# GpSimd's two-input products cut into 256-column pieces, and another order for the second pass of the latent out projection

## The chip, the cores and the metric

The kernel runs on one core of a Trainium2 chip. A core has TensorE (PE, matrix products and transposes), VectorE (DVE), ScalarE (ACT), GpSimd (POOL) and SyncE (SP, which here issues the loads and stores); each works through its own list of instructions and waits for others by semaphores. The metric is the time of one execution on the device in microseconds (us), the median of several.

## The reference

Two transformer blocks of two layers each, in fp32, on 512 tokens of width 1024 (the second block also has 256 context tokens).

```python
# first block: pooling mixer, then stick-breaking attention; after each, x += (p @ ple_w) * sigmoid(x @ ple_gate_w)
u, z = split(rms_norm(x) @ a_w_in)              # windows of 2, 4, 8, 16 tokens over u, minus u
x = x + (einsum(pooled, w_group) * scale * silu(z)) @ a_w_out
k, v = split(rms_norm(x) @ w_kv); q, z = split(rms_norm(x) @ b_w_in)
a[t, s] = beta[t, s] * prod(1 - beta[t, j] for s < j < t)     # beta = sigmoid(q.k / 8), causal
x = x + ((a @ v) * silu(z)) @ b_w_out
# second block: latent attention (layer 0, tokens and context), differential attention (layer 1, tokens only)
shift, scale, gate = adaln(c, ada_w[i], ada_b[i])             # the context has its own, from c_ctx
h = x * (1 + scale) + shift
x = layer_norm(ALPHA * x + gate * (o @ out_w[i]), ln_g[i], ln_b[i])
ctx = layer_norm(ALPHA * ctx + gate_c * (o_c @ out_w[i]), ...)   # in layer 0 alone
```

## The kernel before

**Products and weights.** Every fp32 product is three reduced-precision products: a weight unit of 128 partitions x 1024 columns (512 KB, usually four 128-row slices of the contraction by 256 columns) is loaded into `wraw` (three buffers), ACT casts it to `wh` (L126) and GpSimd subtracts to get the rest `wl` (L127); both have four buffers. `mm3` then issues wh x h, wh x l and wl x h (L147 to L149). `w()` hands out the next unit of a planned list (`plan`) and with that lets the loads run three units and the splits two units ahead. Activations are split the same way: ACT casts, DVE subtracts (L233, L234).

**Stages.** Layer 0 (pooling mixer) runs to about 250 us, the key and value projection to 380, the first block's attention to about 545, the out projection, the latent layer's products and its attention to 1045; the latent out projection with its layer norm (`ln0`) takes the time from 1045 to 1180, differential attention that to 1530, and the last out projection the rest. In the pooling mixer DVE sums windows (L446), scales (L449) and corrects the first tokens (L451); its outputs are the next products' right sides.

**Stick-breaking attention.** Per pair of heads three tiles of scores are made (`first`, L695 on). ACT takes two sigmoids, DVE runs a scan backwards along each segment (L712; a tile of 1024 columns has segments of 512, 384 and 128 columns), GpSimd multiplies the scan by beta (L715, one product of 1023 columns, or two of 255 for the third tile), PE transposes the result (`aT_p`), DVE or ACT evacuates it (`aT`, L733), PE multiplies by the values.

**Latent out projection (`ln0`, L1155; `out_ln`, L1115).** Pass 1 makes the outputs of the context (`c`, two token blocks) and of tokens 0 and 1 (`0`), pass 2 those of tokens 2 and 3 (`1`). Each pass goes through four groups of 256 columns (`cg` 0 to 3), two weight units each, so the same eight units are loaded, cast and split twice. Per group DVE multiplies the sums by the gate (L1140) and adds the residual `r` (L1141, with the row sum); after the last group the layer norm follows (L1147 to L1151, the inverse root in `rsqrt`, L199 to L204). `done` writes tokens back as the residual of the next layer (L1179, L1180; DVE for `0`, GpSimd for `1`). `next_acts` transposes the normalized rows (`hT_p`, two transposes to a 256-column tile), DVE applies the modulation (`hm`, L1189), and `split` makes the next layer's activations `hc`, `h0`, `h1`. For `c` and `0` it is handed to pass 2 as `fill`, called behind each group; for `1` it follows pass 2.

**Gates.** `ada_piece` makes the modulation in 48 small pieces placed through the program; its part 2 writes the gate without bias to DRAM. `gate_rows` (L811 to L818) loads gate and bias, each spread over 128 partitions, and adds them, on GpSimd for the latent layer, on DVE for the last.

**What sets the order.** A scheduler puts each engine's instructions in order ahead of time, by priorities that go by program order, and moves later ones forward where its own model finds an engine waiting. Buffers come from pools with a fixed number of buffers, so a write waits for the last reader of its buffer.

## Time and profile before

| | us |
|---|---|
| median of three runs | 1586.16 (1583.03 to 1586.99) |
| the profiled execution | 1584.99 |
| its span | 1583.2 |
| PE busy in the span | 1488.9 |
| DVE, ACT, POOL busy | 925.2, 733.7, 603.4 |

The profile is of one execution; its span goes from the first to the last instruction, and 1.8 us lie around it. Matmuls overlap in PE's pipeline, so a row's duration of one matmul (0.28 us) is more than the time from one to the next (0.12 us). "Idle" ahead of a row is the time in which the engine had nothing to run, and the name behind the arrow is what it waited for last. [...]

### The profile page before, as it was taken

What the parts mean: (1) busy time and instruction counts of PE and PEld (TensorE: products, weight loads), DVE (VectorE), ACT (ScalarE), POOL (GpSimd) and SP (SyncE); (2) the same over time, 40 slices, a digit from 0 to 9 for tenths busy, and PEclk for the clock granted to TensorE, in tenths of its full rate; (3) what the DMA queues carried; (4) which work ended last, traced back from release to release, by engine and by line L of the source; (5) the groups of instructions that cost most, each with busy time, mean ns of one, the idle gap of its engine ahead of it and who ended that gap; (6) DMA issues with size and microseconds to landing.
All of it is one profiled execution on the core that took longest, in us unless ns stands there. A gap on an engine that the chain in (4) does not pass through costs nothing.

```text
span 1583.2 us, 24444 instructions
## 1 busy us (share of the span) xinstructions
PE 1488.9 (94%) x9590; PEld 1247.9 (79%) x9590; DVE 925.2 (58%) x1769; ACT 733.7 (46%) x1347; POOL 603.4 (38%) x431
## 2 busy tenths in 40 slices
PE   6999999999899899999999999997897999999997
PEld 4777889998555578888876667577797989999987
DVE  6676465532776656442465665547857655555576
ACT  5323344435666433332565555533335553555642
POOL 2533555643544453222333332444342424343310
PEclk9999999999999999999999999999899999999999
DMA  5323432323344334311103030434321112121122
GB/s 168 90 77 93 127 119 75 101 87 98 102 134 134 106 120 124 90 44 50 51 1 116 9 120 2 146 120 164 117 81 44 41 41 68 41 66 43 54 77 97
DMA packets 149747, 136.01 MB, mean 86 GB/s; under 512 B 12612, under 2 KB 135224, under 8 KB 149632
## 3 DMA queue, kind: packets, MB, share of 16 engines
q1 hardware_dynamic: 149632, 134.45, 27.4%
q8 instruction: 76, 1.25, 0.3%
q14 instruction: 39, 0.32, 0.1%
HBM read 126.02 MB, written 8.40 MB: 85 GB/s over the span
## 4 chain that ended last, share of the span: by engine, by line
PE 40%; DVE 7%; ACT 5%; issue 3%; DMA 2%; POOL 1%; SPq 0%; DVEq 0%; POOLq 0%; ACTq 0%
PE PT_p L172 4%; PE pv L1076 3%; PE qkv_p L147 2%; PE qkv_p L149 2%; PE qkv_p L148 2%; PE pv L1440 2%; PE gt_p L147 2%; PE gt_p L148 2%; PE gt_p L149 2%; PE lg L147 2%; PE lg L148 1%; ACT pe L1095 1%; PE lg L149 1%; DVE st L1094 1%; PE ada_p L787 1%
## 5 line engine op out<-in xcount | busy, mean ns | idle before, releaser
L127 POOL TENSOR_TENSOR wl<-wraw,wh 128x1024 fp32r<-128x1024 f32 (+2 forms) x159 | 377.0, 2380 | 377.9 <-ACT wh L126 364.8
L126 ACT CAST wh<-wraw 128x1024 fp32r<-128x1024 f32 (+2 forms) x164 | 166.3, 1020 | 282.1 <-issue 60.7
L1095 ACT ACTIVATE pe<-lg,st 128x768 f32<-128x768 f32 x160 | 130.5, 817 | 71.6 <-DVE st L1094 55.4
L1094 DVE TENSOR_REDUCE st<-lg 128x1 f32<-128x768 f32 x160 | 133.5, 843 | 38.8 <-PE lg L1421 20.1
L1055 POOL TENSOR_SCALAR pe<-pe,st 128x768 f32<-128x768 f32 (+1 forms) x96 | 73.4, 768 | 145.8 <-DVE st L1096 130.1
L147 PE MATMUL qkv_p<-wh,h 128*128 128x256 f32 x384 | 109.5, 285 | 0.9 <-ACT V L1366 0.7
L172 PE MATMUL PT_p<-ident,pe 128*128 128x128 f32 x640 | 99.6, 279 | 9.5 <-DVE pe L1426 3.3
L149 PE MATMUL qkv_p<-wh,h 128*128 128x256 f32 x384 | 108.1, 282 | 0.2 <-DVE h L234 0.2
L148 PE MATMUL qkv_p<-wl,h 128*128 128x256 f32 x384 | 108.1, 282 | 0.0
L172 PEld LDWEIGHTS PT_p<-ident,pe 128*128 128x128 f32 x640 | 72.6, 141 | 39.9 <-issue 16.9
L1425 POOL TENSOR_SCALAR pe<-pe,st 128x768 f32<-128x768 f32 x32 | 29.2, 912 | 126.7 <-DVE st L1424 85.5
L147 PE MATMUL out_p<-wh,o 128*128 128x256 f32 x256 | 74.5, 292 | 0.9 <-DVE y L1292 0.8
L147 PEld LDWEIGHTS qkv_p<-wh,h 128*128 128x128 f32 x384 | 72.5, 189 | 3.4 <-ACT V L1366 1.3
L148 PE MATMUL out_p<-wl,o 128*128 128x256 f32 x256 | 73.7, 290 | 1.4 <-POOL wl L127 1.4
L149 PE MATMUL out_p<-wh,o 128*128 128x256 f32 x256 | 73.5, 291 | 0.1
L147 PE MATMUL kv_p<-wh,kv 128*128 128x256 f32 x256 | 72.2, 282 | 1.2 <-ACT kv L236 1.2
L149 PEld LDWEIGHTS qkv_p<-wh,h 128*128 128x128 f32 x384 | 72.4, 189 | 0.4 <-DVE h L234 0.4
L148 PEld LDWEIGHTS qkv_p<-wl,h 128*128 128x128 f32 x384 | 72.6, 189 | 0.0
L148 PE MATMUL kv_p<-wl,kv 128*128 128x256 f32 x256 | 71.6, 280 | 0.0
L715 POOL TENSOR_TENSOR sb_b<-sb_b,sb_k 128x1023 f32<-128x1023 f32 (+1 forms) x32 | 43.0, 1355 | 74.2 <-DVE sb_k L712 44.9
L149 PE MATMUL kv_p<-wh,kv 128*128 128x256 f32 x256 | 71.2, 280 | 0.0
L712 DVE TENSOR_TENSOR_SCAN sb_k<-sb_k 128x512 f32<-128x512 f32 (+3 forms) x64 | 61.2, 996 | 10.4 <-ACT sb_k L707 10.3
(456 smaller groups left out, 4545.6 us busy)
## 6 DMA issues: line engine op xcount, KB each, us to landing
araw<-in_ada_w_dram SPq DMA_DIRECT2D x48, 512.0 KB
wraw<-in_diff_w_in_dram SPq DMA_DIRECT2D x32, 512.0 KB
wraw<-in_out_w_dram SPq DMA_DIRECT2D x24, 512.0 KB
wraw<-in_a_w_in_dram SPq DMA_DIRECT2D x16, 512.0 KB
...
```

What stands on the lines that cost most here:

```text
L126: nc.scalar.copy(h[:, :n], raw[:, :n])
L127: (nc.vector if i < 3 or pool == "ow3" else nc.gpsimd).tensor_tensor(out=l[:, :n], in0=raw[:, :n], in1=h[:, :n].bitcast(F32), op=ALU.subtract)
L147: mm(out, lhsT=lh, rhs=rh, start=start, stop=False)
L148: mm(out, lhsT=lh, rhs=rl, start=False, stop=False)
L149: mm(out, lhsT=ll, rhs=rh, start=False, stop=stop)
L172: self.nc.tensor.transpose(out, in_, self.ident[:in_.shape[0], :in_.shape[0]])
L712: nc.vector.tensor_tensor_scan(out=kp[:, rev], data0=kp[:, rev], data1=kp[:, rev], initial=1.0, op0=ALU.mult, op1=ALU.min)
L715: nc.gpsimd.tensor_tensor(out=bt[:, o:o + w - 1], in0=bt[:, o:o + w - 1], in1=kp[:, o + 1:o + w], op=ALU.mult)
L1055: nc.gpsimd.tensor_scalar(out=pe, in0=pe, scalar1=st[:, 1:2], scalar2=0.0, op0=ALU.mult, op1=ALU.add)
L1076: return nc.tensor.matmul(pv[64 * ee:64 * ee + 64, :], lhsT=V[:, k0 + k, vs], rhs=HH[px][:, k, :], start=(k == 0), stop=(k == nk - 1))
L1094: nc.vector.tensor_reduce(out=st[:, 0:1], in_=L, axis=AX.X, op=ALU.max, negate=True)
L1095: nc.scalar.activation(pe, L, AF.Exp, bias=st[:, 0:1], accum_out=st[:, 2:3])
```

## The change

It has three parts. (A) A helper `pool_tt` issues a GpSimd two-input operation as pieces of at most 256 columns. It is used for the weight splits (L127), the gate products (L225), a sum of squares (L500) and the stick product (L715); not for GpSimd's other two-input operations (L528, L1000, L1353, L1179, L1180). (B) The gate's bias is loaded into the small row of `ada_piece` and added there by DVE, which copied there before; `gate_rows` keeps only its load. (C) In `ln0` the residual is loaded straight into `y`, the gated sum goes to a small tile `gp`, and `yc`, `y0`, `y1` and the square's target `sq` have buffers of their own. Pass 2 runs through cg 3, 2, 1, 0: the units of cg 3 and 2 are kept from pass 1 (`held`), so 12 units are loaded in place of 16. `fill` now names the group and token block behind which something is called; each call's transposes are tied to that place on PE (`keep_in_program_order`) for all of `c` and the first four chunks of `0`. `hm` is made by ACT. The scaling of `lng` and `lnb` stands in `affine`, called inside pass 1 behind its group 2; since the loop there runs over both streams, it is called twice. The write-back of `0` and `1` moves behind the transposes (`residual`).

```diff
             nc.scalar.copy(h[:, :n], raw[:, :n])
-            (nc.vector if i < 3 or pool == "ow3" else nc.gpsimd).tensor_tensor(out=l[:, :n], in0=raw[:, :n], in1=h[:, :n].bitcast(F32), op=ALU.subtract)
+            if i < 3 or pool == "ow3":
+                nc.vector.tensor_tensor(out=l[:, :n], in0=raw[:, :n], in1=h[:, :n].bitcast(F32), op=ALU.subtract)
+            else:
+                self.pool_tt(l[:, :n], raw[:, :n], h[:, :n].bitcast(F32), ALU.subtract)
             u["hl"] = (self._w_view(h, u["shape"]), self._w_view(l, u["shape"]))
...
+    def pool_tt(self, out, in0, in1, op):
+        for c in range(0, out.shape[1], 256):
+            cs = slice(c, min(c + 256, out.shape[1]))
+            self.nc.gpsimd.tensor_tensor(out=out[:, cs], in0=in0[:, cs], in1=in1[:, cs], op=op)
...
-        self.nc.gpsimd.tensor_tensor(out=out, in0=sg, in1=z, op=ALU.mult)
+        self.pool_tt(out, sg, z, ALU.mult)
...
-                nc.gpsimd.tensor_tensor(out=ssacc, in0=ssacc, in1=sq, op=ALU.add)
+                self.pool_tt(ssacc, ssacc, sq, ALU.add)
...
             for o, w in ((0, 1024),) if len(segs) == 3 else ((0, 256), (512, 256)):
-                nc.gpsimd.tensor_tensor(out=bt[:, o:o + w - 1], in0=bt[:, o:o + w - 1], in1=kp[:, o + 1:o + w], op=ALU.mult)
+                self.pool_tt(bt[:, o:o + w - 1], bt[:, o:o + w - 1], kp[:, o + 1:o + w], ALU.mult)
             if n == 1 and "next" in h:
...
             nc.tensor.matmul(pr[:4, :], lhsT=self.asel, rhs=row[:, :512], start=True, stop=True)
-            nc.vector.tensor_copy(out=row[:4, 512:], in_=pr[:4, :])
+            for b in range(2):
+                nc.sync.dma_start(out=row[2 * b:2 * b + 2, 512:], in_=self.a["ada_b_2"][layer, 2048 + 512 * b:2560 + 512 * b].partition_broadcast(2))
+            nc.vector.tensor_tensor(out=row[:4, 512:], in0=pr[:4, :], in1=row[:4, 512:], op=ALU.add)
             for b in range(2):
...
         g = pool.tile([P, D], F32, name=f"gate{layer}{v}")
-        b = pool.tile([P, D], F32, tag="res_n", name="gate_b")
-        eng = nc.vector if layer else nc.gpsimd
         nc.sync.dma_start(out=g, in_=self.gates[layer, v].rearrange("a b -> (a b)").partition_broadcast(P))
-        nc.sync.dma_start(out=b, in_=self.a["ada_b_2"][layer, 2048:3072].partition_broadcast(P))
-        eng.tensor_tensor(out=g, in0=g, in1=b, op=ALU.add)
         return g
...
             units.append(self.w_cols(WQ, g * 384, 384))
-        for ps in range(2):
-            for cg in range(4):
-                units += self.w_half(a["out_w_2"][0], cg * 256)
+        for cg in (0, 1, 2, 3, 1, 0):
+            units += self.w_half(a["out_w_2"][0], cg * 256)
         return units
...
-    def out_ln(self, streams, pool, done, fill=()):
-        fill = list(fill)
-        per = -(-len(fill) // 4)
+    def out_ln(self, streams, pool, done, cgs, held, fill={}):
...
         for tag, acts, tbs, res, fac, gate in streams:
-            buf = "0" if tag == "0" else "1"
-            y = {t: pool.tile([P, D], F32, tag="y" + buf, name="y" + buf, bufs=len(tbs)) for t in tbs}
-            r = {t: pool.tile([P, D], F32, tag="r" + buf, name="r" + buf, bufs=len(tbs)) for t in tbs}
+            y = {t: pool.tile([P, D], F32, tag="y" + tag, name="y" + tag, bufs=len(tbs)) for t in tbs}
             st = {t: self.small("lnst", 16, 6) for t in tbs}
             for t in tbs:
-                nc.sync.dma_start(out=r[t], in_=res[t * P:(t + 1) * P, :])
-            ys.append((y, r, st))
-        for cg in range(4):
-            ws = [self.w(), self.w()]
+                nc.sync.dma_start(out=y[t], in_=res[t * P:(t + 1) * P, :])
+            ys.append((y, st))
+        for n, cg in enumerate(cgs):
+            ws = held.pop(cg, None) or [self.w(), self.w()]
+            if n >= 2 and cg >= 2:
+                held[cg] = ws
             cs = slice(cg * 256, (cg + 1) * 256)
-            for (tag, acts, tbs, res, fac, gate), (y, r, st) in zip(streams, ys):
+            for (tag, acts, tbs, res, fac, gate), (y, st) in zip(streams, ys):
                 for i in range(0, len(tbs), 2):
...
                     pp = self.p_mm("out_p")
-                    self.tm(ws, acts, pair[0], len(pair), pp, 256)
+                    for j in range(len(pair)):
+                        self.tm(ws, acts, pair[j], 1, pp[:, j * 256:(j + 1) * 256], 256)
+                        for f in fill.get((n, j), ()):
+                            f()
                     for j, t in enumerate(pair):
                         yt = y[t][:, cs]
-                        nc.vector.tensor_tensor(out=yt, in0=pp[:, j * 256:(j + 1) * 256], in1=gate[:, cs], op=ALU.mult)
-                        nc.vector.scalar_tensor_tensor(out=yt, in0=r[t][:, cs], scalar=fac, in1=yt, op0=ALU.mult, op1=ALU.add, accum_out=st[t][:, 4 + cg:5 + cg])
-            for f in fill[cg * per:(cg + 1) * per]:
-                f()
-        for (tag, acts, tbs, res, fac, gate), (y, r, st) in zip(streams, ys):
+                        gp = pool.tile([P, 256], F32, tag="gp", name="gp", bufs=3)
+                        nc.vector.tensor_tensor(out=gp, in0=pp[:, j * 256:(j + 1) * 256], in1=gate[:, cs], op=ALU.mult)
+                        nc.vector.scalar_tensor_tensor(out=yt, in0=yt, scalar=fac, in1=gp, op0=ALU.mult, op1=ALU.add, accum_out=st[t][:, 4 + cg:5 + cg])
+        for (tag, acts, tbs, res, fac, gate), (y, st) in zip(streams, ys):
             for t in tbs:
...
                 nc.vector.tensor_scalar(out=s[:, 1:2], in0=s[:, 0:1], scalar1=-1.0 / D, scalar2=None, op0=ALU.mult)
-                nc.scalar.activation(r[t], y[t], AF.Square, bias=s[:, 1:2], accum_out=s[:, 2:3])
+                sq = pool.tile([P, D], F32, tag="sq", name="sq", bufs=1)
+                nc.scalar.activation(sq, y[t], AF.Square, bias=s[:, 1:2], accum_out=s[:, 2:3])
                 rs = self.rsqrt(s[:, 2:3], 1, 1.0 / D)
...
         lb = pool.tile([P, D], F32, name="lnb")
-        for t, src in ((lg, a["ln_g_2"]), (lb, a["ln_b_2"])):
-            nc.sync.dma_start(out=t, in_=src[0].partition_broadcast(P))
-            nc.gpsimd.tensor_scalar(out=t, in0=t, scalar1=ALPHA, scalar2=0.0, op0=ALU.mult, op1=ALU.add)
+        def affine():
+            for t, src in ((lg, a["ln_g_2"]), (lb, a["ln_b_2"])):
+                nc.sync.dma_start(out=t, in_=src[0].partition_broadcast(P))
+                nc.gpsimd.tensor_scalar(out=t, in0=t, scalar1=ALPHA, scalar2=0.0, op0=ALU.mult, op1=ALU.add)
...
         def done(s, t, y):
-            rows.setdefault(s, []).append(y)
-            if s != "c":
+            rows.setdefault(s, []).append((t, y))
+        def residual(s):
+            for t, y in rows[s]:
                 r = pool.tile([P, D], F32, tag="res_n", name="res_n", bufs=1)
...
-        def next_acts(s, v, dst, res):
+        def next_acts(s, v, dst, res, held=0):
             def chunk(c):
                 pr = self.p_tr("hT_p")[:, :256]
-                for i, y in enumerate(rows[s]):
-                    self.transpose(pr[:, i * P:(i + 1) * P], y[:, c * P:(c + 1) * P])
+                for i, (t, y) in enumerate(rows[s]):
+                    ins = self.nc.tensor.transpose(pr[:, i * P:(i + 1) * P], y[:, c * P:(c + 1) * P], self.ident)
+                    if c < held and i == 0:
+                        self.tc.keep_in_program_order(ins)
                 hm = pool.tile([P, 256], F32, tag="hm2", name="hm2", bufs=3)
-                nc.vector.tensor_scalar(out=hm, in0=pr, scalar1=gs[v][:, c:c + 1], scalar2=bs[v][:, c:c + 1], op0=ALU.mult, op1=ALU.add)
+                nc.scalar.activation(hm, pr, AF.Identity, scale=gs[v][:, c:c + 1], bias=bs[v][:, c:c + 1])
                 res.append(self.split(hm, dst, "h" + s, n=256))
...
         h0, h1, hc = self.h2_acts = [], [], []
-        self.out_ln([("c", oc_acts, [0, 1], a["ctx_2"][0], ALPHA, gc), ("0", o_acts, [0, 1], self.xs, 1.0, gx)], pool, done)
+        held = {}
+        self.out_ln([("c", oc_acts, [0, 1], a["ctx_2"][0], ALPHA, gc), ("0", o_acts, [0, 1], self.xs, 1.0, gx)], pool, done, (0, 1, 2, 3), held, {(2, 0): [affine]})
+        self.w_advance(self.w_next + 3, self.w_next + 2)
         self.plan(self.diff_units())
-        self.out_ln([("1", o_acts, [2, 3], self.xs, 1.0, gx)], pool, done, next_acts("c", 1, "hc2", hc) + next_acts("0", 0, "hx2", h0))
+        fc, f0 = next_acts("c", 1, "hc2", hc, NK), next_acts("0", 0, "hx2", h0, 4)
+        fill = {(1 + i // 2, i % 2): (fc + f0)[2 * i:2 * i + 2] for i in range(6)}
+        self.out_ln([("1", o_acts, [2, 3], self.xs, 1.0, gx)], pool, done, (3, 2, 1, 0), held, fill)
+        for f in f0[4:]:
+            f()
+        residual("0")
         for f in next_acts("1", 0, "hx2", h1):
             f()
+        residual("1")
         self.close("ln0", "og2s")
```

On POOL, where the stick products begin (`sb_b`) behind the last splits (`wl`) of the query and gate weights. Before:

```order
L127 TENSOR_TENSOR wl<-wraw,wh 128x1024 x7
L715 TENSOR_TENSOR sb_b<-sb_b,sb_k 128x1023 x2
L715 TENSOR_TENSOR sb_b<-sb_b,sb_k 128x255
L225 TENSOR_TENSOR og<-sz,og 128x512
L715 TENSOR_TENSOR sb_b<-sb_b,sb_k 128x255
L715 TENSOR_TENSOR sb_b<-sb_b,sb_k 128x1023 x2
```

After (L144 is the line in `pool_tt`):

```order
L144 TENSOR_TENSOR wl<-wraw,wh 128x256 x28
L144 TENSOR_TENSOR sb_b<-sb_b,sb_k 128x256 x3
L144 TENSOR_TENSOR sb_b<-sb_b,sb_k 128x255
L144 TENSOR_TENSOR sb_b<-sb_b,sb_k 128x256 x3
L144 TENSOR_TENSOR sb_b<-sb_b,sb_k 128x255 x2
L144 TENSOR_TENSOR og<-sz,og 128x256
L144 TENSOR_TENSOR sb_b<-sb_b,sb_k 128x255
L144 TENSOR_TENSOR og<-sz,og 128x256
L144 TENSOR_TENSOR sb_b<-sb_b,sb_k 128x256 x3
```

The long product became three pieces of 256 and one of 255 columns, each with its own wait for the scans; a gate product `og` was split in two with a stick product between.

On PE, at transposes of the normalized context rows inside pass 2 (the numbers tell tiles apart; `out_p` is the out projection's sum, `hT_p` the transposes). Before, the first place:

```order
L147 MATMUL out_p_10276<-wh_10266,o_9653 128x256
L148 MATMUL out_p_10276<-wl_10267,o_9653 128x256
L149 MATMUL out_p_10276<-wh_10266,o_9653 128x256
L172 MATMUL hT_p_10329<-ident_99,y1_9710 128x128
L172 MATMUL hT_p_10329<-ident_99,y1_9711 128x128
L172 MATMUL hT_p_10337<-ident_99,y1_9710 128x128
L172 MATMUL hT_p_10337<-ident_99,y1_9711 128x128
L147 MATMUL out_p_10373<-wh_10272,o_9632 128x256
L148 MATMUL out_p_10373<-wl_10273,o_9632 128x256
```

After, the second place:

```order
L158 MATMUL out_p_10719<-wh_10332,o_10016 128x256
L1201 MATMUL hT_p_10784<-ident_99,yc_10063 128x128 [waits Activation_49]
L1201 MATMUL hT_p_10784<-ident_99,yc_10064 128x128
L1201 MATMUL hT_p_10792<-ident_99,yc_10063 128x128 [waits Activation_49]
L1201 MATMUL hT_p_10792<-ident_99,yc_10064 128x128
L156 MATMUL out_p_10919<-wh_10808,o_9995 128x256 [waits Activation_49]
L157 MATMUL out_p_10919<-wl_10809,o_9995 128x256 [waits Pool_49]
L158 MATMUL out_p_10919<-wh_10808,o_9995 128x256
L156 MATMUL out_p_10919<-wh_10808,o_9998 128x256
L157 MATMUL out_p_10919<-wl_10809,o_9998 128x256 [waits Pool_49]
L156 MATMUL out_p_10719<-wh_10477,o_9995 128x256 [waits DVE_49]
L157 MATMUL out_p_10719<-wl_10478,o_9995 128x256
```

Before, the transposes stand behind 48 products of the pass and come again after 11, 30 and 7 products; now the first four stand behind 72, these four behind 24 more, and so on, with the products of cg 1 and 0 behind them. `wl_10809` is a unit of cg 0 and the third that is split after the kept ones; its first five products stand ahead of those of cg 1 (`wl_10478`).

On DVE before, where the first context chunk comes out of the transposes (`hm`, then the subtraction `hc`):

```order
L1151 TENSOR_SCALAR y_9718<-y_9718,lnst,rs_y 128x1024
L204 SCALAR_TENSOR_TENSOR rs_y<-rs_t,rs_y 128x1
L1189 TENSOR_SCALAR hm_10332<-hT_p,gs_9701,bs_9703 128x256
L1179 TENSOR_TENSOR res_n<-y_9718,lng 128x1024
L1151 TENSOR_SCALAR y_9719<-y_9719,lnst,rs_y 128x1024
L1180 TENSOR_TENSOR res_n<-res_n,lnb 128x1024
L234 TENSOR_TENSOR hc<-hm_10332,hc 128x256
L1189 TENSOR_SCALAR hm_10340<-hT_p,gs_9701,bs_9703 128x256
L1189 TENSOR_SCALAR hm_10348<-hT_p,gs_9701,bs_9703 128x256
```

and on ACT after, where that chunk now is:

```order
L126 CAST wh<-wraw 128x1024
L210 ACTIVATE rs_y<-rs_y 128x1
L209 ACTIVATE rs_y<-rs_m 128x1
L126 CAST wh<-wraw 128x1024
L210 ACTIVATE rs_y<-rs_y 128x1
L1205 ACTIVATE hm_10747<-hT_p,bs_10056,gs_10054 128x256
L1205 ACTIVATE hm_10755<-hT_p,bs_10056,gs_10054 128x256
L242 CAST hc<-hm_10747 128x256
L242 CAST hc<-hm_10755 128x256
L126 CAST wh<-wraw 128x1024 x2
```

The evacuation left DVE's list, where residual additions (`res_n`) stood on both sides of it, for ACT's, where it stands behind two weight casts and ahead of two more; the subtraction stays on DVE.

## Rows read from the trace of the kernel before

**Rows 1.** the page's part 1: busy time, share of the span, instructions
```profile
PE 1488.9 (94%) x9590; PEld 1247.9 (79%) x9590; DVE 925.2 (58%) x1769; ACT 733.7 (46%) x1347; POOL 603.4 (38%) x431
```

**Rows 2.** PE's waits: line, waited for: us in total, times, longest us
```profile
PE hT_p L172 <- DVE hm L1189: 12.3, 4, 5.8
PE u_p L147 <- DVE u L441: 5.9, 2, 4.3
PE aT_p L172 <- DVE aT L733: 5.3, 9, 1.5
...
PE z_p L147 <- DVE zr L461: 3.9, 2, 2.6
```

**Rows 3.** stretches: from:to length, busy us (count) by engine, granted PE clock, DMA
```profile
34.30:41.00 6.70, 4.58 (x11) 3.62 (x12) 5.00 (x9) 2.18 (x3) 2.32 (x4) 0.50 0.57 164
426.80:433.50 6.70, 5.38 (x16) 4.41 (x17) 3.81 (x6) 3.80 (x6) 2.12 (x3) 0.50 0.15 57
...
1106.10:1112.80 6.70, 4.81 (x23) 4.82 (x24) 6.06 (x13) 0.41 (x1) 0.24 (x1) 0.50 0.52 182
1119.70:1126.40 6.70, 5.66 (x27) 5.66 (x28) 6.70 (x20) 0.81 (x2) 0.00 (x0) 0.50 0.51 176
...
1519.10:1522.40 3.30, 3.30 (x18) 3.30 (x17) 3.27 (x9) 3.23 (x7) 0.38 (x1) 0.50 0.00 0
...
250.00:380.00 130.00, 129.84 (x1090) 128.57 (x1090) 49.63 (x112) 52.96 (x103) 70.72 (x39) 1.00 0.28 90
...
1092.00:1180.00 88.00, 70.03 (x522) 67.89 (x522) 67.25 (x132) 29.81 (x61) 36.82 (x16) 0.90 0.31 102
```

**Rows 4.** timeline at 1080 to 1089, DVE, POOL: start us, us, operation, count
```profile
1082.97 2.60 DVE L1141 SCALAR_TENSOR_TENSOR y<-r,y 128x256 f32<-128x256 f32 x1
...
1088.07 0.41 DVE L1141 SCALAR_TENSOR_TENSOR y<-r,y 128x256 f32<-128x256 f32 x1
...
1080.35 4.96 POOL L127 TENSOR_TENSOR wl<-wraw,wh 128x1024 fp32r<-128x1024 f32 x2 [2.73 <-ACT wh L126]
```

**Rows 5.** POOL's groups by shape: count, busy us, mean ns, idle time before
```profile
L127 POOL TENSOR_TENSOR wl<-wraw,wh 128x1024 fp32r<-128x1024 f32 x146 | 357.3, 2456 | 331.4 <-ACT wh L126 324.9 <-issue 3.2 <-PE k_p L172 3.0
...
L715 POOL TENSOR_TENSOR sb_b<-sb_b,sb_k 128x1023 f32<-128x1023 f32 x16 | 32.4, 2022 | 60.1 <-DVE sb_k L712 43.5 <-ACT Q L687 8.3 <-PE aT_p L172 3.5
...
L715 POOL TENSOR_TENSOR sb_b<-sb_b,sb_k 128x255 f32<-128x255 f32 x16 | 10.7, 688 | 14.1 <-ACT sb_b L708 7.6 <-PE sb_l L703 5.1 <-DVE sb_k L712 1.4
...
L1353 POOL TENSOR_TENSOR qr<-qr,rt 128x256 f32<-128x256 f32 x12 | 8.8, 738 | 7.2 <-DVE rt L1352 7.2
```

**Rows 6.** timeline at 28 to 37, PE, DVE; [idle time before <- what ended it]
```profile
36.42 0.80 PE L147 MATMUL u_p<-h,wh 128*128 128x512 f32 x1 [4.32 <-DVE u L441]
...
28.93 2.94 DVE L446 TENSOR_TENSOR win<-u 128x527 f32<-128x527 f32 x1
...
33.47 2.29 DVE L451 TENSOR_TENSOR hd<-win,invc 128x2 f32<-128x2 f32 x1
...
36.47 0.71 DVE L446 TENSOR_TENSOR win<-u 128x527 f32<-128x527 f32 x1
```

**Rows 7.** timeline at 423 to 429, PE and DVE
```profile
428.12 1.12 PE L172 MATMUL qT_p<-ident,qtok 128*128 128x128 f32 x4 [3.74 <-DVE aT L733]
...
423.21 4.67 DVE L712 TENSOR_TENSOR_SCAN sb_k<-sb_k 128x256 f32<-128x256 f32 x2
```

**Rows 8.** timeline at 1101 to 1108, PE and DVE
```profile
1107.99 0.69 PE L172 MATMUL hT_p<-ident,y 128*128 128x128 f32 x2 [5.82 <-DVE hm L1189]
...
1101.75 2.31 DVE L202 TENSOR_TENSOR rs_t<-rs_y,rs_m 128x1 f32<-128x1 f32 x1 [0.98 <-ACT rs_y L201]
```

**Rows 9.** timeline at 1117, PE
```profile
1117.17 0.39 PE L148 MATMUL out_p<-wl,o 128*128 128x256 f32 x1 [1.44 <-POOL wl L127]
```

**Rows 10.** timeline at 1518, PE
```profile
1518.08 0.84 PE L172 MATMUL PT_p<-ident,pe 128*128 128x128 f32 x6 [2.23 <-DVE pe L1426]
```

**Rows 11.** timeline at 1544, PE
```profile
1544.47 0.39 PE L147 MATMUL out_p<-wh,o 128*128 128x256 f32 x1 [0.80 <-DVE y L1292]
```

## The prediction

> **What bounds the kernel now.** The first view to read is the page's busy line: TensorE (PE) works for 94% of the span, VectorE (DVE) 58%, ScalarE (ACT) 46%, GpSimd (POOL) 38% [rows 1]. So only the time in which PE stands still or runs slowly can be won: 1583.2 − 1488.9 = 94.3 us outside its matmuls, and on top the stretches at half clock. The second view, PE's waits, says whom it waits for: nearly always DVE, in short transposes, evacuations and scans, although DVE is busy little more than half of the time [rows 2]. [...]
>
> Why DVE is late stands in the fourth view, a timeline of DVE and POOL side by side. DVE's L1141, which reads two SBUF operands, takes 0.41 us at 1088.07 but 2.60 us at 1082.97, where GpSimd is in the second of two tensor_tensor of 128x1024 (1080.35 to 1085.31) [rows 4]. It ends at 1085.57, some 0.3 us behind GpSimd, and it could begin at 1082.97, near the middle of the pair, because the operation ahead of it got its turn there: a DVE operation is held until the running GpSimd instruction is over, then it goes, even where the next GpSimd instruction stands ready. [...] The pause is therefore as long as the rest of a GpSimd instruction, and GpSimd's stand at 2.46 us (146 weight splits) and 2.02 us (16 stick products) [rows 5].
>
> **Part A, GpSimd in quarters.** A wait that lasted the rest of a 2.46 us instruction now lasts the rest of a quarter. Its price: the 255-column product takes 0.688 us [rows 5], so four make 4 × 0.688 = 2.75 us against 2.456, +0.3 us on a weight unit. The bounds are 2.46 us (the split itself is free) and 2.95 (four at 0.738, the rotary product of 256 columns [rows 5]); I take 2.75, since the 255-column product has the same operation and form. Over 146 units that is 44 us of GpSimd time, which lies beside PE: a unit of 48 matmuls keeps PE busy for 48 × 129.84/1090 = 5.72 us in the stage at 250 to 380 [rows 3], twice what four quarters take, and PE reads a unit quarter by quarter (one is 128 rows of the contraction), so that the first is enough to begin. [...]
>
> What it gives, place by place:
> - Layer 0, first group. At 36.42 PE had stood still for 4.32 us for DVE's u; on DVE, L446 lasted 2.94 us at 28.93 and only 0.71 at 36.47, so 2.2 us of it are holding, and an operation on two columns lasted 2.29, nearly all of it holding [rows 6]: some 4.4 us. With quarters each keeps 0.3 to 0.7. I take 3.0 of the 4.32, and the half-clock stretch behind it, 4.58/2 = 2.3 us [rows 3], which follows from the pause: 5.3 (bounds 3 and 5.9).
> - The rest of layer 0: the waits for u and zr, without that pause, are 5.9 + 3.9 − 4.32 = 5.5 us [rows 2]; I take 4 (bounds 2 and 5.5), since PE would also wait a little for the chain of DVE operations itself.
> - Stick-breaking attention: the largest pause, 3.74 us at 428.12, waits for DVE's aT behind two scans of 256 columns that took 4.67 us [rows 7]. I take 3.0 and half of the 5.38 us at half clock [rows 3], 2.7; the other waits for aT, of the transposes that follow, make 5.3 us in nine [rows 2], of which 3.5. That is 9.2. Against it stands a new collision. Before, one product of 1023 columns waits for all its scans; now its quarters start one by one behind the first scan and lie on top of the second and third (a scan reads two SBUF operands). Each of the 16 long products may hold a scan by up to 0.7 us; most of it hides behind PE, and I set it at 2 us (bounds 0 and 16 × 0.7 = 11): 7 in all (−2 to 9.2). That four pieces take 0.7 us longer than the one of 2.02 costs nothing more, since all but the last can be done before the last scan ends.
> - Diff attention: PE waits 2.23 us at 1518.08 for DVE's L1426, an operation with two SBUF inputs [rows 10]; 1.7 of it and half of 3.30 us at half clock [rows 3], 1.65, make 3.3. A weight unit that PE takes as it comes costs 0.3 us more, one of them: 3 (0 to 5).
> - The stage at 250 to 380, where PE is busy for 129.84 of 130 us [rows 3], has nothing to give.
>
> **Part B, gate bias.** The bias goes into a 2x512 row within the modulation pieces (two small loads, a DVE operation in place of a DVE copy); the two 128x1024 additions and two loads per layer go. On GpSimd at the latent layer they were beside the first pass, where PE waits little, so nothing there. At the end PE paused 0.80 us for DVE's y behind the last gate addition [rows 11]; 0.8 (0 to 1.6, twice what is seen).
>
> **Part C, the latent out projection's second pass.** The stage 1092 to 1180 lasts 88 us with PE busy for 70.03 [rows 3], 18.0 us idle, and two half-clock stretches whose matmuls take 4.81 + 5.66 us, half of it lost: 5.2. That is 23.2 us. Where they come from: PE meets the transposes of yc 48 matmuls into the pass, the layer norm's chain isn't done, and the largest pause, 5.82 us at 1107.99, waits for hm behind DVE operations on one column, the first of them held for 2.31 us [rows 8]; hm alone makes 12.3 us of the pauses [rows 2]; a weight half that GpSimd had just split makes 1.44 [rows 9]. After the change PE has 72 matmuls of kept weights (8.6 us at 0.119) ahead of the first transposes, which come in fours with 24 matmuls between; four weight units fewer are loaded, cast and split; the 24 evacuations go from DVE to ACT, on which no row shows a held operation. Residual additions on DVE come behind the transposes rather than between them.
>
> What stays late? First, cg 1's weights are split only when cg 3's have been read, and five matmuls of cg 0 stand ahead of cg 1's: their split is the third after the kept ones, its buffer comes free within the 24 matmuls ahead, and a cast and a quarter stand between: about 2 us of pause (0 to 5). Second, ACT has evacuations and their casts behind two weight casts, about 2 us of delay for the fours at PE, some of it beside the 24 matmuls (2.9 us) between them: 1 us. Third, the layer norm of tokens 2 and 3 at the end still has to be waited for, its square pass, the small operations of the inverse root and the normalization in a row: about 3 us, with perhaps a half-clock stretch behind it. So 7 of 23.2 stay and 16 go (8 to 20). The affine loads run twice (the fill sits in a loop over both streams): two loads and two GpSimd operations more, beside the first pass; nothing.
>
> **Sum**, against the profiled execution's own 1584.99: 5.3 + 4 + 7 + 3 + 0.8 + 16 = 36.1, so 1549. The span is 1583.2, and 1.8 us lie around it in both kernels. The median of the runs is 1.2 above the profiled one: 1550, and so for every case below.
>
> **Rivals.**
> - Rival 1, half the gain: GpSimd's or ACT's queue becomes late for the weights. For it: in the order PE's waits on GpSimd stand at every quarter now, and at ln0 it already waits 1.44 us for one [rows 9]. Against it: four quarters take half of a unit's PE time. Then ln0 gives 8, the stick's collisions take its gain (0), and layer 0, diff and gate 13.1: 1565.
> - Rival 2, all of it: no new wait. Upper bounds 5.9 + 5.5 + 9.2 + 5 + 1.6 + 20 = 47: 1539.
> - Rival 3: GpSimd takes its next quarter ahead of the waiting DVE operation, so that it is held for the whole group as before. Against it speak rows 4, where DVE gets in between two. Then A gives nothing (its price is hidden), ln0 about 12 and the gate 0.8: 1573.
> - Rival 4, slower: a quarter, with DVE's turn behind it, costs GpSimd as much as PE needs for a quarter unit, 5.72/4 = 1.43 us. From there POOL sets the pace wherever units follow each other at 48 matmuls (kv 16, PLE gates 16, mixer 24, attention's out product 8: 64 units). At 1.6 us a unit is 6.4, +0.7 × 64 = 45 us, with 25 of the gains left: 1606. Rows 5 are against it: a quarter's like take 0.69 to 0.74.
>
> **How the numbers follow.** Forecast (1540 to 1561) 0.60; rival 1 0.20; rival 2 0.08; rival 3 0.04; rival 4 0.05; an unforeseen wait that eats all of it, 0.03. The predicted time is the forecast's, 1550. The range for 8 in 10 is 1535 to 1573: it leaves out rival 4, half of rival 3 and a few per cent at either end. About 0.3%, 4.8 us, is what a measurement of this kernel can tell from no change; the forecast and rivals 1 to 3 lie beyond that on the fast side. Their sum is faster 0.92, same 0.03 (the unforeseen wait), slower 0.05 (rival 4).
>
> **What would show it.** DVE operations of 1.5 to 3 us beside POOL should be gone (L446 at 28.93 below 1.4); the half clock behind 36, 428 and 1518 should be gone; POOL's 256-column pieces should average 0.6 to 0.74 us; PE's waits for hm should fall from 12.3 to under 4, and the stage of the second pass from 88 to about 72 us. It would be wrong if pieces came at 1 us or more, if scans of the stick lasted longer in sum than before, or if PE's waits for POOL's wl (1.44 before [rows 9]) came to more than 10.

## The result and the profile after

The changed kernel takes 1563.7 us (median, 1561.91 to 1566.66) against 1585.2 for the one before on the same chip: a ratio of 0.9861, with a 95% interval of 0.9842 to 0.9880. That is 21.5 us gained where 36 were forecast; 1563.7 lies inside the range, nearest to rival 1 (1565).

The page of the kernel after: part 1, and from part 5 the largest group (count | busy us, mean ns | idle before it).

```profile
PE 1483.1 (95%) x9590; PEld 1244.0 (80%) x9590; DVE 857.1 (55%) x1744; ACT 739.6 (47%) x1367; POOL 712.7 (46%) x933
...
L144 POOL TENSOR_TENSOR wl<-wraw,wh 128x256 fp32r<-128x256 f32 x598 | 465.8, 813 | 345.5 <-ACT wh L126 330.3
```

Beside [rows 1], DVE is busy for 68 us less: shorter holds (L446 over 527 columns of u fell from 1.45 to 0.96 us in the mean), and the evacuations and additions that left it. POOL is busy for 109 us more. One piece of a weight split takes 0.813 us in the mean, so a unit is 4 × 0.813 = 3.25 us, not the 2.75 of the forecast nor the 2.95 of its upper bound.

PE's waits after (line, waited for: us in total, times, longest us):

```profile
PE aT_p L181 <- DVE aT L742: 5.7, 10, 1.8
PE hT_p L1201 <- DVE y L1160: 4.2, 1, 4.2
...
PE out_p L157 <- POOL wl L144: 3.9, 1, 3.9
...
PE u_p L156 <- DVE u L450: 2.7, 2, 1.3
...
PE hT_p L1201 <- ACT hm L1205: 2.6, 3, 1.4
...
PE mix_p L156 <- DVE zr L480: 2.3, 1, 2.3
```

Beside [rows 2], the 12.3 us for DVE's `hm` are gone (2.6 for ACT's), u and zr are smaller, aT is the same (in sum u and zr fell from 11.7 to 6.2 us, although the wait for zr at `mix_p` rose from 1.9 to 2.3). New in this size are a wait for `wl` of 3.9 us in one piece (1.44 before [rows 9]) and one of 4.2 us in one piece for the layer norm's `y` (3.1 us in two before). A wait of 2.6 us for a load, at 135, is new too and is shown further below. The waits for `wl` and `y` have a granted clock of 0.50 behind them (share of full speed; windows: length, PE, PEld, DVE, ACT, POOL busy, granted clock, DMA):

```profile
239.40:242.80 3.40, 3.40 (x17) 3.40 (x17) 1.04 (x7) 0.41 (x2) 0.00 (x0) 0.50 0.30 110
522.70:526.10 3.40, 3.40 (x18) 1.90 (x15) 1.28 (x2) 0.00 (x0) 2.83 (x5) 0.50 0.00 0
1099.60:1106.40 6.80, 6.13 (x27) 5.97 (x28) 5.12 (x10) 0.21 (x1) 6.80 (x8) 0.50 0.74 231
1130.30:1133.70 3.40, 3.29 (x16) 3.29 (x17) 1.82 (x3) 2.18 (x5) 1.62 (x1) 0.50 0.34 135
```

The granted clock is 0.50 in each, as in [rows 3]. In the first of them one matmul of 256 columns follows the next after 0.213 us (240.0 to 242.6), and after 0.119 at a clock of 1.00 (the same products, 244.6 to 248.0); with 512 columns it is 0.426 (before, 37.4 to 40.4) and 0.233 (after, 33.7 to 37.9). So 44 to 45% of the matmuls' time in such a stretch is what the clock of 0.50 costs: up to 1.5 us in 3.4. The stretches behind 36, 428 and 1518 are gone, as forecast; those at 239, 1099 and 1130 are in other places than before. At the differential layer's start two such stretches (1188.3 to 1195.2 and 1202.0 to 1205.4) stand where before there was one (1208.4 to 1215.2).

**Where the time went.** The same PE instruction stands in both traces, so the difference of its times is what was gained up to there. The table has these differences by stretch, in us (negative: faster than before), for all kernels of this study that are discussed below, each from its one profiled execution. The stretches end, in the kernel before, at 298 (the key and value projection), 571 (behind the first attention), 1096 (pass 2 of the latent out projection, 36 products in, counted from the pass's start since the order of its groups differs), 1189 (the differential layer's first products), and at PE's last instruction.

| kernel | median, us | 0–298 | 298–571 | 571–1096 | 1096–1189 | rest |
|---|---|---|---|---|---|---|
| the change | 1563.7 | −4.1 | −3.5 | −0.4 | −10.2 | −3.5 |
| forecast of it | 1550 | −9.3 | −7 | 0 | −16 | −3.8 |
| quarters alone (A) | 1570.0 | −3.8 | −2.6 | +0.2 | −7.4 | −2.1 |
| new order and gates alone (B, C) | 1582.6 | +2.6 | −2.4 | +1.2 | −2.2 | −2.2 |
| halves | 1566.9 | −3.5 | −6.0 | +0.1 | −3.5 | −2.8 |
| eighths | 1585.4 | +1.3 | −5.0 | +2.7 | +1.9 | −2.0 |
| write-back in quarters too | 1558.8 | −3.1 | −5.2 | +1.2 | −16.9 | −4.9 |
| stick product whole | 1563.7 | −1.0 | −5.3 | −0.6 | −10.3 | −3.3 |
| write-back late, on DVE | 1554.8 | −3.0 | −3.4 | +0.4 | −21.1 | −3.0 |
| splits on DVE | 1545.6 | −14.5 | +0.3 | −0.9 | −23.3 | −0.1 |
| kernel before, splits on DVE | 1560.3 | −16.2 | +5.0 | −0.6 | −12.3 | +0.1 |
| splits and late write-back on DVE | 1544.8 | −14.8 | −1.3 | −2.0 | −23.4 | +0.2 |
| the same, other products in halves | 1546.4 | −15.4 | +1.9 | +1.6 | −22.9 | −1.0 |

How far such a difference can be trusted is seen at two kernels. The one with the write-back in quarters is the change itself up to 1096, and yet its stretches differ from the change's by 1.0, 1.7 and 1.6 us. The one with the stick product whole has the change's instructions up to 383 us, and yet its first stretch differs by 3.1 us; a half-clock stretch from 137.7 to 141.1, which the change does not have, is up to 1.5 of them. Differences of 3 us or less in one stretch say nothing. With splits on DVE the gain at the end ("rest") is offset by longer half-clock stretches at the differential layer's start (in the change with splits on DVE 13.7 us from 1165.0, against 6.8 before).

### The profile page after: what moved, and what is told of

The parts are those of the page before. It is cut to its first block, busy times and chain, and to the rows that moved or that the text cites. A ratio compares the mean times of both kernels' runs of the same rounds, so it can differ in the third digit from the quotient of the medians.

```text
span 1561.6 us, 25009 instructions
## 1 busy us (share of the span) xinstructions
PE 1483.1 (95%) x9590; PEld 1244.0 (80%) x9590; DVE 857.1 (55%) x1744; ACT 739.6 (47%) x1367; POOL 712.7 (46%) x933
## 3 DMA queue, kind: packets, MB, share of 16 engines
q8 instruction: 76, 1.25, 0.3%
## 4 chain that ended last, share of the span: by engine, by line
PE 41%; ACT 5%; DVE 5%; issue 4%; POOL 2%; DMA 1%; POOLq 0%; DVEq 0%; SPq 0%; ACTq 0%
PE PT_p L181 4%; PE qkv_p L156 3%; PE pv L1083 3%; PE qkv_p L158 3%; PE qkv_p L157 3%; PE gt_p L156 2%; PE gt_p L157 2%; PE gt_p L158 2%; PE pv L1464 2%; PE lg L156 2%; ACT pe L1102 2%; PE lg L157 1%; PE lg L158 1%; DVE st L1101 1%; PE ada_p L796 1%
## 5 line engine op out<-in xcount | busy, mean ns | idle before, releaser
L144 POOL TENSOR_TENSOR wl<-wraw,wh 128x256 fp32r<-128x256 f32 x598 | 465.8, 813 | 345.5 <-ACT wh L126 330.3
L126 ACT CAST wh<-wraw 128x1024 fp32r<-128x1024 f32 (+2 forms) x160 | 162.1, 1019 | 280.0 <-issue 38.8
L181 PEld LDWEIGHTS PT_p<-ident,pe 128*128 128x128 f32 x640 | 72.6, 141 | 38.0 <-issue 17.6
L144 POOL TENSOR_TENSOR sb_b<-sb_b,sb_k 128x256 f32<-128x256 f32 (+1 forms) x80 | 59.4, 770 | 46.4 <-ACT sb_b L717 23.5
L721 DVE TENSOR_TENSOR_SCAN sb_k<-sb_k 128x512 f32<-128x512 f32 (+3 forms) x64 | 59.6, 972 | 10.5 <-ACT sb_k L716 10.3
```

The costliest lines, as they stand in the source:

```text
L126: nc.scalar.copy(h[:, :n], raw[:, :n])
L144: self.nc.gpsimd.tensor_tensor(out=out[:, cs], in0=in0[:, cs], in1=in1[:, cs], op=op)
L181: self.nc.tensor.transpose(out, in_, self.ident[:in_.shape[0], :in_.shape[0]])
L721: nc.vector.tensor_tensor_scan(out=kp[:, rev], data0=kp[:, rev], data1=kp[:, rev], initial=1.0, op0=ALU.mult, op1=ALU.min)
```

## The experiments

Each ratio is against the kernel before, measured again beside that run (medians 1583.9 to 1586.6 us), so a difference of two kernels' medians is good to a few us.

**Quarters alone.** The kernel before with `pool_tt` in the four places of part A and nothing else.

> Part A alone (quarters on GpSimd; old second pass, old gates). Theory 1 (the pauses outside the second pass are held DVE operations, and its own are half held operations, half order): layer 0, stick-breaking and differential attention give the 4.1, 3.3 and about 2 us that the whole change gives there, the second pass 3 to 6: about 1571 us, ratio 0.990 to 0.993. Rival (the second pass is held operations alone): 18 us, 1567. Rival (quarters give nothing without the new order): 1585.

Measured: 1570.0 us, 0.9902 (0.9886 to 0.9918). Theory 1, with more in the second pass (7.4 us) than it said. Quarters alone make 15 of the 21.5 us.

**The new order alone.** The change with `pool_tt` in one piece:

```diff
-        for c in range(0, out.shape[1], 256):
-            cs = slice(c, min(c + 256, out.shape[1]))
+        for c in range(0, out.shape[1], 1024):
+            cs = slice(c, min(c + 1024, out.shape[1]))
```

> Parts B and C with whole GpSimd operations. Theory 1: the second pass gives 4 to 7 us and the end 1: about 1578 us, ratio 0.994 to 0.997. Rival (the new order is what helps and quarters only feed the queue of the weights): 10 us and more in the second pass, 1574 or less. If the parts add up, the gains of this run and of the quarters alone make the change's 21.5 us.

Measured: 1582.6 us, 0.9984 (0.9969 to 0.9999); a gain of 2.5 us, less than either theory allowed. The two parts alone make 15.1 + 2.5 = 17.6 us of the 21.5; the other 4 us are within the three intervals (each some 2.5 to 3 us to either side), so it is not shown that the parts help each other. The timeline of this kernel at its second pass (start us, us, engine, line; first DVE, last row PE) shows why the order is worth so little alone:

```profile
1099.58 2.36 DVE L211 TENSOR_TENSOR rs_t<-rs_y,rs_m 128x1 f32<-128x1 f32 x1
...
1102.20 2.10 DVE L212 SCALAR_TENSOR_TENSOR rs_t<-rs_t,rs_y 128x1 f32<-128x1 f32 x1
...
1104.98 2.84 DVE L1160 TENSOR_SCALAR y<-y,lnst,rs_y 128x1024 f32<-128x1024 f32 x1
...
1113.88 0.75 DVE L1150 TENSOR_TENSOR gp<-out_p,gate 128x256 f32<-128x256 f32 x2
...
1114.68 0.58 PE L156 MATMUL out_p<-wh,o 128*128 128x256 f32 x1 [6.73 <-DVE gp L1150]
```

Two DVE operations on one column last 2.36 and 2.10 us and a normalization 2.84, each beside whole weight splits (2.46 us in the mean in this kernel); so the gated sum `gp`, for which PE waits 6.73 us, begins only at 1113.88. The new order still met a late DVE there.

**Halves and eighths.** The same two lines with 512 and with 128.

> The whole change with pieces of 512 columns. Theory 1 (a hold as long as the rest of a piece is what counts): DVE waits up to 1.3 us in place of 0.7, so layer 0 and the stick lose about half of their gain, 1567 us (4 above the change). Rival (GpSimd's longer queue in the second pass, pieces at 0.8 to 1.1 us, is what the quarters lost): the unit is cheaper, the 3.9 us wait for weights in the second pass shrinks, and the time is at or below the change's, 1563 or less.

> The whole change with pieces of 128 columns. Theory 1: holds shrink to 0.35 us, but a unit grows from 3.25 to some 4.2 us and more with DVE's turns between (a piece of 128 columns in the rotary product takes 0.46); weights become late in the second pass and in places elsewhere: 1565 to 1575 us. Rival (only the hold's length counts): faster than the change, 1558 to 1561.

Measured: halves 1566.9 us, 0.9879 (0.9861 to 0.9898); eighths 1585.4, 1.0008 (0.9991 to 1.0026). Halves land where theory 1 put them, but their interval overlaps that of the change, so quarters against halves is not decided for the whole. In the second pass halves give only 3.5 us; PE's waits in that kernel show a pause for a gated sum again, 6.8 us in one piece where the whole operations had 6.7:

```profile
PE out_p L156 <- DVE gp L1150: 7.1, 2, 6.8
```

Eighths give all of it back, more than theory 1 said. A piece of 128 columns (POOL's groups by shape, then PE's waits in this kernel):

```profile
L144 POOL TENSOR_TENSOR wl<-wraw,wh 128x128 fp32r<-128x128 f32 x1196 | 575.2, 521 | 293.1 <-ACT wh L126 280.5 <-PE o_p L156 7.1 <-PE k_p L181 3.0
```

```profile
PE qkv_p L156 <- DVE rt L1376: 6.0, 2, 5.9
PE out_p L157 <- POOL wl L144: 5.6, 1, 5.6
```

A unit takes 8 × 0.521 = 4.17 us, and PE waits 5.6 us in one piece for `wl` in the second pass, 1.7 more than in the change, where a unit takes 3.25. The largest wait, for the rotary product `rt`, has another cause (DVE, POOL, PE):

```profile
1174.37 6.66 DVE L1377 TENSOR_TENSOR kr<-kr,rt 128x256 f32<-128x256 f32 x1
...
1171.56 9.19 POOL L144 TENSOR_TENSOR wl<-wraw,wh 128x128 fp32r<-128x128 f32 x22
...
1181.48 0.58 PE L156 MATMUL qkv_p<-wh,h 128*128 128x256 f32 x1 [5.88 <-DVE rt L1376]
```

A DVE operation of 256 columns, 0.43 us undisturbed, lasts 6.66 us, across 15 whole pieces of GpSimd. So here DVE got no turn between pieces, which is rival 3 of the prediction. It happened once more in this trace (4.44 us at 596.36, across nine pieces) and in no other trace of this study: in none of them does a DVE operation last across more than one whole two-input operation of GpSimd (the longest such one 3.19 us before, 2.37 in the change). Why it happens with these pieces, and then only twice, the runs do not show. The late weights and this hold are seen; the eighths' other losses, 5.4 us of them in the first stretch, were not all traced.

**The write-back.** GpSimd also multiplies and adds 128x1024 rows for tokens 2 and 3 (`residual`), which the change left whole. In the change's own trace, behind the second pass (POOL, DVE, PE):

```profile
1124.35 2.38 POOL L1193 TENSOR_TENSOR res_n<-y,lng 128x1024 f32<-128x1024 f32 x1 [1.54 <-DVE rs_t L211]
...
1124.37 2.37 DVE L212 SCALAR_TENSOR_TENSOR rs_t<-rs_t,rs_y 128x1 f32<-128x1 f32 x1
...
1127.00 2.29 DVE L213 SCALAR_TENSOR_TENSOR rs_y<-rs_t,rs_y 128x1 f32<-128x1 f32 x1
...
1130.41 0.69 PE L1201 MATMUL hT_p<-ident,y 128*128 128x128 f32 x2 [4.16 <-DVE y L1160]
```

Two operations of one column last 2.37 and 2.29 us, each until a write-back product ends (at 1126.73 and 1129.28), and the layer norm's last rows, for which PE waits 4.16 us, come behind them. The experiment cuts these four products as well:

```diff
-                eng.tensor_tensor(out=r, in0=y, in1=lg, op=ALU.mult)
-                eng.tensor_tensor(out=r, in0=r, in1=lb, op=ALU.add)
+                if s == "1":
+                    self.pool_tt(r, y, lg, ALU.mult)
+                    self.pool_tt(r, r, lb, ALU.add)
+                else: ...
```

> The change, with GpSimd's write-back products of tokens 2 and 3 (four operations of 128x1024 that the change left whole) in quarters too. Theory (PE's 4.2 us pause at 1130 is two DVE operations of one column held behind them for 2.4 and 2.3 us, and the half clock and later waits follow from it): 3 to 5 us faster than the change, 1559 to 1561. Rival (that pause is the layer norm's own chain): same as the change, 1563 to 1565.

Measured: 1558.8 us, 0.9833 (0.9799 to 0.9867), 4.9 us under the change's median. The interval overlaps the change's a little, but the second pass is 6.7 us better in the table; some 1.5 of these are a shorter half-clock stretch at 1101 (3.4 us in place of 6.8), ahead of the first instruction that the edit touches, and some 5 us, clear of what one execution can err by, are left to the edit. In its trace the two operations and PE's pause have shrunk, as the theory said (DVE, then PE):

```profile
1124.51 0.73 DVE L212 SCALAR_TENSOR_TENSOR rs_t<-rs_t,rs_y 128x1 f32<-128x1 f32 x1
...
1125.50 0.69 DVE L213 SCALAR_TENSOR_TENSOR rs_y<-rs_t,rs_y 128x1 f32<-128x1 f32 x1
...
1127.71 0.44 PE L1205 MATMUL hT_p<-ident,y 128*128 128x128 f32 x2 [1.32 <-DVE y L1160]
```

**Write-back on DVE, behind the next layer's activations.** Here nothing of the write-back stands on GpSimd, nor on DVE ahead of the second pass's sums (`last_sub` is the latest subtraction that `split` gave to DVE):

```diff
-                r = pool.tile([P, D], F32, tag="res_n", name="res_n", bufs=1)
-                eng = nc.gpsimd if s == "1" else nc.vector
-                eng.tensor_tensor(out=r, in0=y, in1=lg, op=ALU.mult)
+                r = pool.tile([P, D], F32, tag="res_n", name="res_n", bufs=3)
+                eng = nc.vector
+                self.behind(eng.tensor_tensor(out=r, in0=y, in1=lg, op=ALU.mult), self.last_sub)
...
-        residual("0")
         for f in next_acts("1", 0, "hx2", h1):
             f()
+        residual("0")
         residual("1")
```

> The change, with all write-back products (tokens 0 to 3) on DVE behind the last activation of the next layer, three buffers for them: DVE is free for the gated sums at 1100 and nothing of GpSimd holds the layer norm at 1124. Theory: both large pauses of the second pass (3.9 and 4.2 us, with 6.8 and 3.4 us at half clock behind them) shrink; 5 to 9 us faster than the change, 1555 to 1559. Rival (the first pause is GpSimd's queue of weights, which isn't touched): 3 to 4 us, 1560. Risk: the rotary products of the next layer come behind 10 us of writes on DVE, which could cost 5 us, 1563 or more.

Measured: 1554.8 us, 0.9804 (0.9776 to 0.9833), 9 us under the change, as much as the theory allowed, with the second pass at −21.1. So the change's first pause there is not GpSimd's list alone. The change's rows at that place (POOL, PE, DVE):

```profile
1090.19 16.36 POOL L144 TENSOR_TENSOR wl<-wraw,wh 128x256 fp32r<-128x256 f32 x16 [18.95 <-ACT wh L126]
...
1100.27 0.58 PE L157 MATMUL out_p<-wl,o 128*128 128x256 f32 x1 [3.88 <-POOL wl L144]
...
1100.42 0.74 DVE L1150 TENSOR_TENSOR gp<-out_p,gate 128x256 f32<-128x256 f32 x2
```

Sixteen pieces follow each other for 16.36 us, 1.02 us a piece: the first two take 0.74 us each, the next three 0.99 to 1.19 beside DVE's operations. The longer pieces stand beside the write-back products of a block of tokens (POOL's fifth to seventh piece, then DVE):

```profile
1093.48 4.67 POOL L144 TENSOR_TENSOR wl<-wraw,wh 128x256 fp32r<-128x256 f32 x3
...
1094.61 1.21 DVE L1193 TENSOR_TENSOR res_n<-y,lng 128x1024 f32<-128x1024 f32 x1
...
1096.35 1.21 DVE L1194 TENSOR_TENSOR res_n<-res_n,lnb 128x1024 f32<-128x1024 f32 x1
```

The sixth and the seventh take 1.78 and 1.77 us, against 0.74 at the same place in the kernel with the late write-back: here GpSimd's pieces last longer beside DVE. The ninth, the first of the third unit, ends at 1100.21, and PE, which goes on at 1100.27, had waited 3.88 us for it. Without these products on DVE the pause falls to 1.56 us; PE then stops once more, for 0.47 us, for the gated sum that frees the sum's buffer.

**Stick product whole.** The change with L715's product as it was.

> The change, with the stick product whole again (quarters elsewhere). Theory 1 (quarters that start behind the first scan collide with the next scans and cost what they save): within 2 us of the change, 1562 to 1566, with scans no longer in sum. Rival (the held scans of before were held by these products): the stage of the stick loses its 3.3 us, 1567. The run with halves gained 5.6 us there, so a gain of some 2 us by whole products would say that the quarters' collisions cost that much.

Measured: 1563.7 us, 0.9857 (0.9823 to 0.9890), the change's own time. Cutting the stick product neither gains nor costs anything that can be measured here. The pause of 3.74 us at 428 [rows 7] is 1.25 us in the change, 1.19 with the stick product whole and 3.75 with the new order alone, so what shortens it is the cutting of GpSimd's other operations. (The stretch's sums, −3.5, −5.3 and −2.4 us, are too near to each other to say more.) Of the new collision that the prediction priced at 2 us, and at up to 11, a little is seen on DVE and nothing in the time: the 64 scans take 59.6 us in the change's trace, 57.6 with whole products, 61.2 before.

**Splits on DVE.** All weight splits go to DVE, whole (`if i < 3 or pool == "ow3":` becomes `if True:`).

> The change, with all weight splits on DVE, whole, as the first three units have it: GpSimd then has few two-input operations left to hold DVE with, and DVE has about 155 more operations of 1.2 us, 185 us. Theory (holding is what cost the time): DVE at 65% of the span with no held operations; pauses of short waits behind a 1.2 us split remain: 1560 to 1575 us, well under the kernel before. Rival (DVE's own load is what counts, the holds only a part of it): 1585 or more.

Measured: 1545.6 us, 0.9745 (0.9716 to 0.9774), 18 us under the change and beyond the best that was expected. Its part 1 of the page, and DVE's timeline at the place of [rows 6]:

```profile
PE 1481.7 (96%) x9590; PEld 1240.2 (80%) x9590; DVE 946.5 (61%) x1899; ACT 738.7 (48%) x1367; POOL 260.8 (17%) x335
```

```profile
29.89 0.71 DVE L455 TENSOR_TENSOR win<-u 128x527 f32<-128x527 f32 x1
30.51 1.22 DVE L128 TENSOR_TENSOR wl<-wraw,wh 128x1024 fp32r<-128x1024 f32 x1
31.65 0.68 DVE L458 SCALAR_TENSOR_TENSOR pl<-win,u 128x512 f32<-128x512 f32 x1
32.25 0.15 DVE L460 TENSOR_TENSOR hd<-win,invc 128x2 f32<-128x2 f32 x1
```

DVE takes a split in 1.22 us where GpSimd took 2.46, and does the rest at this place at its undisturbed length: L455 0.71 us, two columns 0.15. It is busy for 61% in place of 55%, POOL for 17%. (The scheduler plans the order anew for this, so other places move a little too.) Holds are not gone everywhere: in the second pass DVE's `h` still takes 2.2 to 2.6 us beside each of GpSimd's whole write-back products, but PE does not wait for it. Layer 0 gains 14.5 us, more than three times what quarters gave. The shorter split is not what does it: before, PE waited 0.5 us for `wl` in this stretch and 11.7 us for DVE's u and zr. With quarters 6.2 us of the latter stay; with the splits on DVE none do, and the half clock at 36 and at 239 is absent as well.

**What the new order is worth without holds.** The kernel before with its splits on DVE.

> The kernel before (old second pass, old gates, whole stick products) with all weight splits on DVE. It gives what the new second pass is worth where nearly nothing is held: the change with the same splits ran at 1545.6. Theory (the order's worth was hidden by held operations on both sides, and counts in full without them): the old order's second pass still meets its transposes 48 products in, waits for the layer norm and holds the write-back: 8 to 15 us more than that, 1554 to 1560. Rival (the order is worth 2 to 3 us, as it was with whole GpSimd operations): 1548.

Measured: 1560.3 us, 0.9843 (0.9814 to 0.9871), 14.7 us slower than the change with the same splits. In the second pass the order is worth 23.3 − 12.3 = 11 us here; with quarters 10.2 − 7.4 = 2.8; with whole operations 2.2. The largest of PE's pauses in this kernel's second pass:

```profile
1101.32 0.58 PE L147 MATMUL out_p<-wh,o 128*128 128x256 f32 x1 [4.60 <-DVE y L1140]
```

The old order still waits, now on its own account, 4.6 us for a gated sum that stands behind the layer norm and the write-back on DVE, and the clock is 0.50 from 1095.3 to 1105.6. Between the two profiled executions 4.7 us more lie in stretch 298–571, where this kernel also has the stick products whole; that part was not followed.

**Both together.** Splits and late write-back on DVE, and the same with GpSimd's remaining products in halves.

> The change with weight splits on DVE and write-backs on DVE behind the next layer's last activation. Theory: the two gains overlap in the second pass, where the splits on DVE left pauses of 0.95 and 1.37 us: 0 to 3 us better than the splits alone, 1543 to 1546. Rival (they add up in full, 9 us): 1537. Rival (DVE's list is now too long there): 1548 or more.

> As the kernel above, and GpSimd's remaining products (stick, gate, sum of squares) in halves of 512 columns in place of quarters. In the stick's stage halves gave 2.3 us more than quarters where splits were GpSimd's too. Theory (fewer starts on top of running scans): 1 to 3 us better than the kernel above. Rival (that was the shorter queue behind splits): no difference, within 1 us.

Measured: 1544.8 us, 0.9749 (0.9710 to 0.9788), and 1546.4, 0.9747 (0.9710 to 0.9784). Neither differs from the splits on DVE alone. The two gains overlap: with splits on DVE there was little left in the second pass for the write-back to spoil. And the better stretch 298–571 of the halves above is not repeated here, so it is no effect of halves that these runs could show (−1.3 and +1.9 us).

## Why the prediction was right, and which terms were off

The sign and the range held, and so did the mechanism where it was looked at: the pauses at 36, 428 and 1518, behind DVE operations that whole GpSimd instructions had held, fell from 4.32, 3.74 and 2.23 us to 1.31, 1.25 and 0.60, and the half clock behind them is gone. They are not most of what PE loses: the time outside its matmuls was 94.3 us before, 78.5 after, and is 63.0 with the splits on DVE.

The forecast's own band, 1540 to 1561, was missed by 2.7 us; the time came out at rival 1's number. That they agree is in part luck: rival 1 had 8 us for the second pass, 0 for the stick and 13.1 for the rest, and measured are 10.2, 3.5 and 7.6. Its mechanism, weights that come late, is seen in one pause (3.9 us at 1100), but not in the sizes it gave. Rival 3 (no turn between pieces) and rival 4 (a piece at 1.43 us in the mean) did not happen with pieces of 256 columns. Of the signs that the prediction named, two failed: the pieces average 0.813 us, not 0.6 to 0.74, and the second pass, between the same instructions, fell from 93.3 to 83.2 us and not by 16. The size was off by some 15 us, in three terms. Beside these, the sum counts half of the matmuls' time at a clock of 0.50 as lost (2.3, 2.7, 1.65 and 5.2 us); no run shows a half, the traces show 44 to 45%, so these terms were about a tenth too large.

- **Layer 0: 9.3 forecast, 4.1 measured.** The holds gave nearly what they were priced at: the pause at 36.42 fell by 3.0 us, as forecast, the half clock behind it went (some 2.1, for 2.3), and the three other pauses for u and zr in the sum fell from 5.5 to 2.5 us, 3.0 of the 4. DVE is still held a little at the place of [rows 6] (DVE, POOL, PE):

```profile
29.46 1.30 DVE L455 TENSOR_TENSOR win<-u 128x527 f32<-128x527 f32 x1
30.79 1.11 DVE L458 SCALAR_TENSOR_TENSOR pl<-win,u 128x512 f32<-128x512 f32 x1
31.83 0.67 DVE L460 TENSOR_TENSOR hd<-win,invc 128x2 f32<-128x2 f32 x1
...
29.45 5.58 POOL L144 TENSOR_TENSOR wl<-wraw,wh 128x256 fp32r<-128x256 f32 x6 [3.34 <-ACT wh L126]
...
33.16 0.50 PE L156 MATMUL u_p<-h,wh 128*128 128x512 f32 x1 [1.31 <-DVE u L450]
```

  These three operations take 3.08 us, where they take 1.54 without holds; the 1.31 us of pause that stay are what the forecast had left. What failed is a term that the sum put at nothing: new waits in this stage. The largest is for a load (SyncE, PE):

```profile
130.89 0.37 SPq L116 DMA_DIRECT2D wraw<-in_a_w_out_dram  x1
131.35 1.95 SPq L337 DMA_DIRECT2D p_tok<-in_p_dram  x4
...
135.47 0.41 PE L181 MATMUL pT_p<-ident,p_tok 128*128 128x128 f32 x2 [2.61 <-DMA p_tok<-in_p_dram]
```

  The weight load ahead of `p_tok` in SyncE's list waits for its buffer until a split ends on GpSimd at 130.86, so `p_tok` is issued at 131.35 and later, and PE comes to the transposes at 132.86. Before, PE stood still for 2.58 us, for zr, shortly ahead of this place, and not here; with halves it stands 1.37 us there and 1.25 here, with quarters not there and 2.6 to 2.9 us here: what the shorter hold gave back, this load took. With the splits on DVE PE has neither wait. Further, PE waits 0.9 us longer for ACT's first h and 0.5 for the zr of `mix_p`, and loses 1.5 us to the half clock at 239; the pauses for kv and for wl, shorter or gone, give 1.5 back. (The 4.1 is of one execution; the one with the stick product whole, equal up to there, has 1.0.)

- **Second pass: 16 forecast, 10.2 measured.** The forecast gave it to the order. The runs show that the order alone is worth 2.2 us there, quarters alone 7.4, both 10.2, and the order 11 only where little is held. The step that failed is "what stays late". It priced the third split unit at 2 us and took 0.69 to 0.74 us for its pieces, where they took 1.02 beside DVE's operations; PE waited 3.9 us. It put ACT's evacuations at 1 us; PE waited 2.6 us for them. It put the layer norm at 3 us and did not see that GpSimd's write-back products, left whole, would hold it; PE waited 4.2 us. And it left about 1 us for half clock, where the two stretches have 6.13 and 3.29 us of matmuls in them: 4.7 counted by half as in the forecast, 4.2 at the measured share. So 15.4 us stayed by its own count, and not 7. On the other side the trace of before has a third half-clock stretch in this stage (1140.2 to 1143.5, 3.21 us of matmuls) that the 23.2 us left out. Cutting the write-back products gave 4.9 us in the median.

- **Stick: 7 forecast, 3.5 measured.** The pause at 428 gave 2.5 of its 3.0 us and the half clock behind it went (some 2.4, for 2.7). The 3.5 us set on the other waits for aT did not come: they are 5.7 us in ten [rows 2: 5.3 in nine], and 8.2 in ten with the splits on DVE, so shorter holds do not shorten them. What would is open. The collision that was set against it cost nothing that can be seen in the time.

The price of the quarters was the other mis-sized term: 3.25 us a unit against 2.75. It cost nothing that can be seen between 571 and 1096, as forecast, and made the weights late in the second pass. The rest came as forecast, as far as one execution can tell: the differential layer and the end gave 3.5 us for 3.8, with both pauses smaller (PE):

```profile
1497.89 0.84 PE L181 MATMUL PT_p<-ident,pe 128*128 128x128 f32 x6 [0.60 <-DVE pe L1450]
...
1519.65 0.39 PE L156 MATMUL out_p<-wh,o 128*128 128x256 f32 x1 [0.48 <-DVE y L1316]
```

The first was 2.23 us [rows 10], the second 0.80 [rows 11], so the gate is worth 0.3 us of the 0.8 that it was given.
